# 304 transposes of a decoder layer move from TensorE to VectorE, in squares of 32 by 32

## The chip, the cores and the metric

The kernel runs on one core of a Trainium2 chip. The metric is the device time of one execution in microseconds. In the profile TensorE is PE (its loads of the stationary operand are PEld), VectorE is DVE, ScalarE is ACT, GpSimd is POOL, SyncE is SP.

## What is computed

One decoder layer in float32: 256 tokens, 2048 features, a feed-forward width of 5632, two attentions of 8 heads with 128 features each.

```python
x = x + 0.5 * swiglu(rmsnorm(x, g_ffn1), w_ffn1_gu, w_ffn1_down)
h = rmsnorm(x, g_mix)
qa, ka, va, qb, kb, vb, gate_a, gate_b = split(h @ w_in)
o_a = diff_attention(qa, ka, va)       # attention 1, two softmax maps per head
o_b = moba_attention(qb, kb, vb)       # attention 2; with 256 tokens plain causal attention
merged = sigmoid(gate_a) * (o_a @ p_a) + sigmoid(gate_b) * (o_b @ p_b)
x = x + merged @ w_o
x = x + 0.5 * swiglu(rmsnorm(x, g_ffn2), w_ffn2_gu, w_ffn2_down)
return rmsnorm(x, g_final)
# swiglu(h): gate, up = split(h @ w_gu); (silu(gate) * up) @ w_down
```

## The kernel before

All weights are read once, from DRAM, in pieces `raw` of 512 rows by 512 columns (three buffers). A float32 product is made of three passes of TensorE: a number is split into a high and a low part of 12 bits each, and hi x hi, hi x lo and lo x hi are added up in PSUM. So each piece of weights is split on the chip, two blocks of 128 rows at a time: ACT makes `wh` (line 102), DVE makes `wl` (line 103), each in four buffers. Activations are the stationary operand: 128 features by 128 tokens, split in the same way, and for that they must be transposed, with the features on the partitions.

`products` (line 122) runs one product: for every 128 rows k of the weights and for both token tiles t it issues three matmuls of 512 columns (lines 130 to 132). Its two PSUM tiles `acc` are two of four, so that the next product can run while the last one is read out. For each pair of row blocks PE issues 12 matmuls, ACT one wh, DVE one wl.

What comes out of a product has the tokens on the partitions. To be an operand again it goes through `flipped` (line 172): TensorE transposes four blocks of 128 by 128 into a PSUM tile `tr`, and ACT and DVE split that into the operand. There are three forms. `put` (line 180) writes hi and lo of h (the feed-forward's inner activations, 22 blocks of 512 columns in all) and of mg (the merged attentions, 4 blocks). `put_x` (line 202) does it for x with a gain, 4 blocks for each of three operands. `put_rows` (line 198) writes the queries and keys of an attention (qk, 4 blocks for each), ACT alone. Such a piece of work is for both token tiles, so eight transposes. It isn't done at once: it is put into the queue `work`, and `products` takes one piece out of it after each 512 rows of weights from the second on (line 141). The stages of the attention heads stand in the same queue.

The stages follow each other: the first feed-forward (gate and up of six blocks, a down product over these, five blocks, a down product over those, which also ends each block of x), q, k, v of attention 1, the same of attention 2 with the heads of attention 1 in between, two gates of 2048 columns with the heads of attention 2 in between, then `merged` in 4 blocks (lines 412 to 424: a product with p_a and one with p_b of 8 row blocks each, multiplied by the gates on DVE, line 419, and added, line 423), `w_o` in 4 products (line 425), and the second feed-forward. A block of x is ready when its last product has been added (lines 261 and 428); `after` then queues its transposes.

A scheduler writes each engine's order of instructions before the run, by priorities and by when it expects an instruction to be ready. The splits of weights are given a priority 600 instructions ahead (line 151).

Of the kernel before, what the change touches and what calls it, by code (L numbers as in the profile page):

```python
"""One decoder layer: SwiGLU half-step, differential and MoBA attention in parallel, SwiGLU
half-step, RMSNorm.

Products with weights: a float32 number is the exact sum of two float32r numbers of 12 significant
bits each, so x @ w is hi(x) @ hi(w) + hi(x) @ lo(w) + lo(x) @ hi(w) + lo(x) @ lo(w) with exact
products. The first three are passes of TensorE at its full rate; the last is at most 2**-24 of
each product, under the rounding of a float32 product, as is the error of a product that leaves it
out. Activations are stationary (transposed, 128 tokens by 128), weights stream past them in blocks
of 512 columns, are split on the chip, and each is read from DRAM once.

An RMSNorm's gain is applied as the rows are transposed and its 1/rms to the product, which is
linear in each row.
"""
# [14 lines left out]
ALU = mybir.AluOpType  # L28
# [8 lines left out]
NB = 512  # L37
HEADS = 8
# [8 lines left out]
def layer(ctx: ExitStack, tc: tile.TileContext, x_in, g_ffn1, w_gu1, w_down1, g_mix, w_in, lam_q1,  # L47
# [12 lines left out]
    # the activation functions of the SwiGLU are loaded before anything waits for them  # L60
# [8 lines left out]
    def load_gains(c0, gs):  # L69
        """A column of `gains` for each 128 features of the gains."""  # L70
        n = sum(g.shape[-1] for g in gs) // P
        rows = tp.tile([n, P], F32, name="gain_rows", tag="osq", bufs=1)
        r = 0
        for g in gs:
            m = g.shape[-1] // P
            nc.scalar.dma_start(rows[r:r + m], g[0].rearrange("(k p) -> k p", p=P))
            r += m
        tr = psum.tile([P, n], F32, name="tr_g", tag="tr", bufs=2)
        nc.tensor.transpose(tr, rows, ident[:n, :n])
        return nc.vector.tensor_copy(gains[:, c0:c0 + n], tr).ins  # L80
# [5 lines left out]
    def make_dist():  # L86
        # key position - query position where that is <= 0, a large negative number elsewhere:
        # queries 0..127 with keys 0..127, then queries 128..255 with keys 0..255
        nc.gpsimd.iota(dist[:, :P], pattern=[[1, P]], base=0, channel_multiplier=-1,
                       allow_small_or_imprecise_dtypes=True)  # L90
        nc.gpsimd.iota(dist[:, P:], pattern=[[1, S]], base=-P, channel_multiplier=-1,
                       allow_small_or_imprecise_dtypes=True)
        nc.gpsimd.affine_select(dist[:, :P], dist[:, :P], pattern=[[-1, P]], compare_op=ALU.is_ge, fill=NEG,
                                base=0, channel_multiplier=1)
        nc.gpsimd.affine_select(dist[:, P:], dist[:, P:], pattern=[[-1, S]], compare_op=ALU.is_ge, fill=NEG,
                                base=P, channel_multiplier=1)

# [1 line left out]
    def split(hi, lo, src, scale=None):  # L99
        """src (* scale) as hi + lo, exactly."""  # L100
        if scale is None:
            a = nc.scalar.activation(hi, src, AF.Copy)  # L102
            b = nc.vector.tensor_tensor(lo, src, hi.bitcast(F32), op=ALU.subtract)  # L103
        else:
            a = nc.scalar.activation(hi, src, AF.Copy, scale=scale)  # L105
            b = nc.vector.scalar_tensor_tensor(lo, src, scale, hi.bitcast(F32), op0=ALU.mult, op1=ALU.subtract)
        return a.ins, b.ins

    def after_all(instructions):
        """What follows is issued behind these on their engines."""  # L110
        stack = ExitStack()
        for i in instructions:
            stack.enter_context(tc.issue_after(i))
        return stack
# [7 lines left out]
    def products(lhs, w, starts, nk, before=None, behind=(), apart=0):  # L122
        """For each n0 of starts two PSUM tiles, 128 tokens each: lhs (an operand) @ w[:, n0:n0+512].
        The last `apart` rows of 128 go through TensorE for one token tile, then for the other.
        Other work that waits goes in between, a piece for each 512 rows."""
# [9 lines left out]
        for c in range(0, nk, 4):  # L135
# [6 lines left out]
            for i, (acc, n0) in enumerate(zip(accs, starts)):  # L142
# [5 lines left out]
                for b in range(0, 4, 2):  # L148
                    wh = wp.tile([P, 2, NB], F32R, name="wh", bufs=4)
                    wl = wp.tile([P, 2, NB], F32R, name="wl", bufs=4)  # L150
                    with tc.high_priority(offset=PRIORITY), after_all(begun if c == 0 else ()):
                        pair = split(wh, wl, raw[:, b:b + 2, :])
                    if fill is not None and c == b == i == 0:
                        with after_all(pair):
                            begun.extend(fill())
                    for j in range(2):
                        k = c + b + j
                        last = passes(acc, 0, k, wh[:, j, :], wl[:, j, :])
                        if k < nk - apart:
                            passes(acc, 1, k, wh[:, j, :], wl[:, j, :])  # L160
                        else:
                            later.append((acc, 1, k, wh[:, j, :], wl[:, j, :]))
# [9 lines left out]
    def flipped(src):  # L172
        """[128, up to 4 * 128] in PSUM: each 128 columns of src, transposed."""
# [6 lines left out]
    def put(lhs, k0, srcs):  # L180
        """Columns of the token tiles go transposed, as hi + lo, into an operand."""
        for t, src in enumerate(srcs):
            n = src.shape[-1] // P
            tr = flipped(src).rearrange("p (k q) -> p k q", k=n)
            hi, lo = columns(lhs, k0, n, t)
            split(hi, lo, tr)

    def operand(nk, *tags):
        """Tokens' rows, transposed, in one piece for each tag: (hi, lo), each [128, nk, 256]."""
        return [tuple(keep.tile([P, nk, S], F32R, name=f"{tag}{i}", tag=f"{tag}{i}") for i in "hl") for tag in tags]  # L190

    def columns(lhs, k, n, t):
        """n times 128 columns of a token tile, as hi and lo: [128, n, 128]."""
# [4 lines left out]
    def put_rows(dst, srcs):  # L198
        for t, src in enumerate(srcs):
            nc.scalar.activation(dst[:, :, t * P:(t + 1) * P], flipped(src).rearrange("p (k q) -> p k q", k=4), AF.Copy)  # L200

    def put_x(lhs, n0, g):
        """x[:, n0:n0+512] * gain, transposed."""
# [13 lines left out]
    def inverse_rms(ss):  # L217
        """1 / rms of each row, [128, 1] for each token tile."""
# [14 lines left out]
    def ffn(xT, ss, w_gu, w_down, after, before=None, behind=(), apart=0):  # L233
        rstd = None
        parts = [range(0, 6), range(6, 11)]
        for part, blocks in enumerate(parts):
            hT = operand(24, "big")
            for b in blocks:
# [12 lines left out]
                hs = []  # L251
                for t in range(T):
                    hs.append(tp.tile([P, NB], F32, name="h", tag="h", bufs=2))
                    nc.vector.scalar_tensor_tensor(hs[t], up[t], rstd[t], sg[t], op0=ALU.mult, op1=ALU.mult)
                work.appendleft(partial(put, hT, (b - blocks[0]) * 4, hs))
# [11 lines left out]
    def weights(h, maps, qT, kT):  # L267
        """p: [128, maps, 384], queries 0..127 then 128..255; their sums: [128, 2, maps]."""
# [20 lines left out]
    def flip_weights(a):  # L289
        """[128 keys, 384]: keys 0..127 for all queries, keys 128..255 for queries 128..255."""  # L290
# [4 lines left out]
    def diff_head(h, qT, kT, v, lam, on, oT):  # L295
# [3 lines left out]
        # (p0 - p1 * lam * sum0 / sum1) is the difference of the maps times sum0  # L299
# [46 lines left out]
    def qkv(xT, rstd, n0, dim, tag):  # L346
        """Transposed queries (scaled) and keys [128, head, 256], values [128, token tile, 1024]."""
# [7 lines left out]
        for i, (dst, r) in enumerate(((qT, rq), (kT, rstd))):  # L355
            for b in range(W // NB):
                y = product(xT, w_in[0], n0 + i * W + b * NB, KD)
                hs = []
                for t in range(T):
                    hs.append(tp.tile([P, NB], F32, name="qk", tag="h", bufs=2))  # L360
                    nc.vector.tensor_scalar(hs[t], y[t], r[t], None, op0=ALU.mult)
                work.appendleft(partial(put_rows, dst[:, 4 * b:4 * b + 4], hs))
# [6 lines left out]
    def lam_of():  # L369
# [7 lines left out]
        # -lam  # L377
# [4 lines left out]
    def in_steps(heads):  # L382
        """A stage of each head after the same stage of the head before; a step takes the next stage
        of every head under way."""
# [8 lines left out]
    def mixer(xT, ss, after):  # L393
# [18 lines left out]
        for n0 in range(0, D, NB):  # L412
# [7 lines left out]
            hs = []  # L420
            for t in range(T):
                hs.append(tp.tile([P, NB], F32, name="mg", tag="h", bufs=2))
                nc.vector.tensor_add(hs[t], gates[0][:, t, cols], gates[1][:, t, cols])
            work.appendleft(partial(put, mT, n0 // P, hs))
# [12 lines left out]
    def next_operand(g, nk, *tags):  # L437
        """What the step before fills: the operand, and the sums of squares."""
        lhs, ss = [], square_sums()

        def after(n0):
            if not lhs:
                lhs.extend(operand(nk, *tags))
            sum_squares(ss, n0)
            work.appendleft(partial(put_x, lhs, n0, g))
# [6 lines left out]
    def load_x(k):  # L452
        """Starts the load of 512 columns; the function that puts them into the operand."""
# [69 lines left out]
```

## Time and profile before

| | |
|---|---|
| time, median of 3 runs (lowest to highest) | 2143.42 us (2143.32 to 2143.74) |
| the profiled execution, first to last instruction | 2141.3 us |
| PE, weight loads PEld busy | 2124.6 us, 1760.1 us |
| DVE, ACT busy | 1116.9 us, 981.2 us |
| granted clock of PE, mean | 0.999 of 2.4 GHz |

The numbers come from one profiled execution; the page gives the busy time of each engine and the groups of instructions, and other views of the same trace give them in order of time. A record of PE ends where the last result has left the array, so records of neighbours overlap, and what an instruction costs PE is read from start to start. In a row of a group, the last part is the idle time of the engine just ahead of these instructions and what ended it.

### The profile page before, as it was taken

How to read it: one execution, taken by the hardware profiler on the slowest of the kernel's cores; microseconds unless marked ns; L12 is line 12 of the kernel's file. 1: busy time of each engine (PE TensorE's matmuls, PEld its weight loads, DVE VectorE, ACT ScalarE, POOL GpSimd, SP SyncE). 2: the span in 40 equal slices, each digit the busy share in tenths (PEclk: the TensorE clock that was granted, in tenths of full speed). 3: DMA queues.
4: the chain of work that ended last, by engine and by line, in shares of the span. 5: the costliest groups of instructions: out<-in, count | busy, mean ns of one | idle time of the engine just before them, and what ended most of it. 6: DMA issues, size and time to landing. Idle time of an engine off the chain costs nothing.

```text
span 2141.3 us, 23791 instructions
## 1 busy us (share of the span) xinstructions
PE 2124.6 (99%) x9634; PEld 1760.1 (82%) x9634; DVE 1116.9 (52%) x1238; ACT 981.2 (46%) x1224; POOL 11.7 (1%) x26
## 2 busy tenths in 40 slices
PE   8999999999999999999999999999999999999998
PEld 7888888888888888778888888888888888888886
DVE  5554454454555554665554466555554545445554
ACT  6444433344444444555564544544444433444443
POOL 0000000000000000000000000000000000000000
PEclk9999999999999999999999999999999999999999
DMA  7555555555555555544545555566555555555553
GB/s 259 187 186 195 183 192 197 195 184 191 196 183 191 183 190 178 176 157 158 180 162 189 196 187 187 188 205 196 179 195 190 186 195 196 191 185 195 192 184 136
DMA packets 201792, 401.20 MB, mean 187 GB/s; under 512 B 6945, under 2 KB 6994, under 8 KB 201554
## 3 DMA queue, kind: packets, MB, share of 16 engines
q1 hardware_dynamic: 201584, 399.66, 56.2%
q8 instruction: 75, 1.23, 0.2%
q14 instruction: 35, 0.29, 0.0%
q10 hardware_dynamic: 98, 0.03, 0.0%
HBM read 397.57 MB, written 2.10 MB: 187 GB/s over the span
## 4 chain that ended last, share of the span: by engine, by line
PE 99%; ACT 1%; DMA 0%; DVE 0%; ACTq 0%; issue 0%; SPq 0%; POOLq 0%
PE acc L130 32%; PE acc L132 32%; PE acc L131 32%; PE tr L177 2%; ACT wh L102 0%; DMA raw<-in_w_ffn_gu_dram 0%; PE sc L274 0%; PE o L341 0%; PE sc L272 0%; ACT on L316 0%; ACT oah L105 0%; PE o L342 0%; DVE wl L103 0%; DVE s L277 0%; SPq L456 0%
## 5 line engine op out<-in xcount | busy, mean ns | idle before, releaser
L103 DVE TENSOR_TENSOR wl<-raw,wh 128x1024 fp32r<-128x1024 f32 x752 | 921.3, 1226 | 988.0 <-ACT wh L102 987.6
L102 ACT ACTIVATE wh<-raw 128x1024 fp32r<-128x1024 f32 x752 | 796.7, 1060 | 1070.1 <-PE acc L132 1039.9
L130 PE MATMUL acc<-wh,xTh 128*128 128x512 f32 x1472 | 578.3, 393 | 2.0 <-ACT xTh L105 2.0
L132 PE MATMUL acc<-wh,xTl 128*128 128x512 f32 x1472 | 574.1, 390 | 0.0
L131 PE MATMUL acc<-wl,xTh 128*128 128x512 f32 x1472 | 573.6, 390 | 0.0
L130 PEld LDWEIGHTS acc<-wh,xTh 128*128 128x128 f32 x1472 | 276.9, 188 | 59.4 <-ACT xTh L105 2.4
L132 PEld LDWEIGHTS acc<-wh,xTl 128*128 128x128 f32 x1472 | 276.7, 188 | 58.0
L131 PEld LDWEIGHTS acc<-wl,xTh 128*128 128x128 f32 x1472 | 277.0, 188 | 56.3
L130 PE MATMUL acc<-wh,bigh 128*128 128x512 f32 x704 | 274.5, 390 | 0.0
L132 PE MATMUL acc<-wh,bigl 128*128 128x512 f32 x704 | 274.0, 389 | 0.0
L131 PE MATMUL acc<-wl,bigh 128*128 128x512 f32 x704 | 273.9, 389 | 0.0
L130 PE MATMUL acc<-wh,oah 128*128 128x512 f32 x416 | 163.1, 392 | 0.0
L132 PE MATMUL acc<-wh,oal 128*128 128x512 f32 x416 | 162.0, 390 | 0.0
L131 PE MATMUL acc<-wl,oah 128*128 128x512 f32 x416 | 161.9, 389 | 0.0
L130 PE MATMUL acc<-wh,obh 128*128 128x512 f32 x416 | 161.8, 389 | 0.0
L131 PE MATMUL acc<-wl,obh 128*128 128x512 f32 x416 | 161.8, 389 | 0.0
L132 PE MATMUL acc<-wh,obl 128*128 128x512 f32 x416 | 161.8, 389 | 0.0
L131 PEld LDWEIGHTS acc<-wl,bigh 128*128 128x128 f32 x704 | 132.2, 188 | 27.4
L132 PEld LDWEIGHTS acc<-wh,bigl 128*128 128x128 f32 x704 | 132.1, 188 | 27.4
L130 PEld LDWEIGHTS acc<-wh,bigh 128*128 128x128 f32 x704 | 132.2, 188 | 27.2
L132 PEld LDWEIGHTS acc<-wh,oal 128*128 128x128 f32 x416 | 78.1, 188 | 16.4
L130 PEld LDWEIGHTS acc<-wh,obh 128*128 128x128 f32 x416 | 78.1, 188 | 16.2
(112 smaller groups left out, 927.1 us busy)
## 6 DMA issues: line engine op xcount, KB each, us to landing
raw<-in_w_ffn_gu_dram SPq DMA_DIRECT2D x174, 1024.0 KB, 5.0
raw<-in_w_ffn_down_dram SPq DMA_DIRECT2D x88, 1024.0 KB, 5.0
raw<-in_w_in_dram SPq DMA_DIRECT2D x80, 1024.0 KB, 5.1
raw<-in_w_o_dram SPq DMA_DIRECT2D x16, 1024.0 KB, 5.0
raw<-in_p_a_dram SPq DMA_DIRECT2D x8, 1024.0 KB, 5.1
raw<-in_p_b_dram SPq DMA_DIRECT2D x8, 1024.0 KB, 5.0
x<-in_x_dram SPq DMA_DIRECT2D x8, 256.0 KB, 5.4
raw<-in_w_ffn_gu_dram SPq DMA_DIRECT2D x4, 512.0 KB, 6.1
```

Source lines behind the costliest of these rows:

```text
L102: a = nc.scalar.activation(hi, src, AF.Copy)
L103: b = nc.vector.tensor_tensor(lo, src, hi.bitcast(F32), op=ALU.subtract)
L130: nc.tensor.matmul(acc[t], hi, wh, start=(k == 0), stop=False)
L131: nc.tensor.matmul(acc[t], hi, wl, start=False, stop=False)
L132: return nc.tensor.matmul(acc[t], lo, wh, start=False, stop=(k == nk - 1)).ins
L177: nc.tensor.transpose(tr[:, i * P:(i + 1) * P], src[:, i * P:(i + 1) * P], ident)
```

## The change

`turned` does the transposes of a block of 512 columns on VectorE: 16 instructions, one for each quarter a of the tokens' 128 partitions and each quarter c of the features' 128. Each reads 32 partitions of both token tiles, 256 numbers of each partition, and transposes them in squares of 32 by 32; it writes the 32 partitions of the features. The result `rows` lies in SBUF with its columns in the order a, t, block, token, and the splits read it in an order that puts them right. `turned` is called where the block is made; only the splits wait in `work`. The two token tiles of a block are now one tile `hs` with one buffer, in place of two buffers of one tile each, `rows` has one buffer, and `wl` has three buffers in place of four.

The first operand (the x that is loaded) still goes through `put_x` and TensorE. The queries and keys go through `turned` where nothing waits in `work`, else through `flipped`: at attention 1 the queue is empty, at attention 2 the heads of attention 1 wait in it.

```diff
+Q = 32
...
-                    wl = wp.tile([P, 2, NB], F32R, name="wl", bufs=4)
+                    wl = wp.tile([P, 2, NB], F32R, name="wl", bufs=3)
...
-    def put(lhs, k0, srcs):
-        for t, src in enumerate(srcs):
-            n = src.shape[-1] // P
-            tr = flipped(src).rearrange("p (k q) -> p k q", k=n)
-            hi, lo = columns(lhs, k0, n, t)
-            split(hi, lo, tr)
+    def both_tiles(name):
+        return tp.tile([P, T, NB], F32, name=name, tag="h", bufs=1)
+
+    def turned(both):
+        rows = tp.tile([P, 4, T, 4, Q], F32, name="rows", tag="rows", bufs=1)
+        both = both.rearrange("p t (k c j) -> p c t k j", c=4, j=Q)
+        for a in range(4):
+            for c in range(4):
+                nc.vector.transpose(rows[c * Q:(c + 1) * Q, a], both[a * Q:(a + 1) * Q, c])
+        return rows
+
+    def put(lhs, k0, rows):
+        for t in range(T):
+            hi, lo = (part.rearrange("p k (a i) -> p k a i", i=Q) for part in columns(lhs, k0, 4, t))
+            split(hi, lo, rows[:, :, t].rearrange("p a k i -> p k a i"))
...
+    def put_turned_rows(dst, rows):
+        for t in range(T):
+            nc.scalar.activation(dst[:, :, t * P:(t + 1) * P].rearrange("p k (a i) -> p k a i", i=Q),
+                                 rows[:, :, t].rearrange("p a k i -> p k a i"), AF.Copy)
+
+    def put_turned(lhs, n0, g, rows):
+        for i in range(NB // P):
+            k = n0 // P + i
+            for t in range(T):
+                hi, lo = (part[:, 0].rearrange("p (a i) -> p a i", i=Q) for part in columns(lhs, k, 1, t))
+                split(hi, lo, rows[:, :, t, i], scale=gains[:, g * KD + k:g * KD + k + 1])
...
-                hs = []
-                for t in range(T):
-                    hs.append(tp.tile([P, NB], F32, name="h", tag="h", bufs=2))
-                    nc.vector.scalar_tensor_tensor(hs[t], up[t], rstd[t], sg[t], op0=ALU.mult, op1=ALU.mult)
-                work.appendleft(partial(put, hT, (b - blocks[0]) * 4, hs))
+                hs = both_tiles("h")
+                for t in range(T):
+                    nc.vector.scalar_tensor_tensor(hs[:, t], up[t], rstd[t], sg[t], op0=ALU.mult, op1=ALU.mult)
+                work.appendleft(partial(put, hT, (b - blocks[0]) * 4, turned(hs)))
...
-                work.appendleft(partial(put_rows, dst[:, 4 * b:4 * b + 4], hs))
+                if work:
+                    put_piece = partial(put_rows, dst[:, 4 * b:4 * b + 4], hs)
+                else:
+                    put_piece = partial(put_turned_rows, dst[:, 4 * b:4 * b + 4], turned(hs))
+                work.appendleft(put_piece)
...
-            work.appendleft(partial(put, mT, n0 // P, hs))
+            work.appendleft(partial(put, mT, n0 // P, turned(hs)))
...
+            rows = turned(x[:, :, n0:n0 + NB])
             sum_squares(ss, n0)
-            work.appendleft(partial(put_x, lhs, n0, g))
+            work.appendleft(partial(put_turned, lhs, n0, g, rows))
```

## Rows read from the trace of the kernel before

**Rows 1.** The page: span, busy time of each engine, chain that ended last.

```profile
span 2141.3 us, 23791 instructions
...
PE 2124.6 (99%) x9634; PEld 1760.1 (82%) x9634; DVE 1116.9 (52%) x1238; ACT 981.2 (46%) x1224; POOL 11.7 (1%) x26
...
PE 99%; ACT 1%; DMA 0%; DVE 0%; ACTq 0%; issue 0%; SPq 0%; POOLq 0%
```

**Rows 2.** Groups by line: count | busy us, mean ns | idle before, releaser.

```profile
L103 DVE TENSOR_TENSOR wl<-raw,wh 128x1024 fp32r<-128x1024 f32 x752 | 921.3, 1226 | 988.0 <-ACT wh L102 987.6
L102 ACT ACTIVATE wh<-raw 128x1024 fp32r<-128x1024 f32 x752 | 796.7, 1060 | 1070.1 <-PE acc L132 1039.9 <-issue 18.6 <-ACT sq L215 5.3
```

**Rows 3.** PE in order of time, around eight transposes: start, length, what.

```profile
106.59 0.40 PE L132 MATMUL acc<-wh,xTl 128*128 128x512 f32 x1
106.82 1.04 PE L177 MATMUL tr<-ident,h 128*128 128x128 f32 x8
...
107.93 0.39 PE L131 MATMUL acc<-wl,xTh 128*128 128x512 f32 x1
```

**Rows 4.** Groups by line: PE's transposes that the change touches.

```profile
L177 PE MATMUL tr<-ident,h 128*128 128x128 f32 x176 | 22.8, 272 | 0.0
...
L177 PE MATMUL tr<-ident,x 128*128 128x128 f32 x96 | 13.4, 285 | 0.0
...
L177 PE MATMUL tr<-ident,qk 128*128 128x128 f32 x64 | 8.3, 272 | 0.0
...
L177 PE MATMUL tr<-ident,mg 128*128 128x128 f32 x32 | 4.1, 272 | 0.0
```

**Rows 5.** Groups by line: prices on DVE, and one on ACT.

```profile
L254 DVE SCALAR_TENSOR_TENSOR h<-acc,rstd,sg 128x512 f32<-128x512 f32 x44 | 31.0, 743 | 0.2 <-issue 0.2
...
L103 DVE TENSOR_TENSOR bigl<-tr,bigh 128x512 fp32r<-128x512 f32 x44 | 28.2, 682 | 0.0
...
L106 DVE SCALAR_TENSOR_TENSOR xTl<-tr,gains,xTh 128x128 fp32r<-128x128 f32 x64 | 20.3, 346 | 3.5 <-ACT xTh L105 3.4
...
L416 ACT ACTIVATE gate<-gate 128x512 f32<-128x512 f32 x16 | 10.1, 634 | 0.4
...
L304 DVE SCALAR_TENSOR_TENSOR a<-s,c 128x256 f32<-128x256 f32 x8 | 3.8, 479 | 0.0
...
L103 DVE TENSOR_TENSOR obl<-o,obh 128x256 fp32r<-128x256 f32 x8 | 3.3, 418 | 0.0
...
L335 DVE TENSOR_SCALAR a<-s,inv 128x256 f32<-128x256 f32 x8 | 2.8, 348 | 0.0
```

**Rows 6.** DVE in order of time, an h block.

```profile
99.95 1.23 DVE L103 TENSOR_TENSOR wl<-raw,wh 128x1024 fp32r<-128x1024 f32 x1 [1.50 <-ACT wh L102]
101.09 1.40 DVE L254 SCALAR_TENSOR_TENSOR h<-acc,rstd,sg 128x512 f32<-128x512 f32 x2
102.67 1.23 DVE L103 TENSOR_TENSOR wl<-raw,wh 128x1024 fp32r<-128x1024 f32 x1 [0.18 <-ACT wh L102]
```

**Rows 7.** DVE in order of time, end of an mg block.

```profile
1267.04 1.28 DVE L419 TENSOR_TENSOR gate<-acc,gate 128x512 f32<-128x512 f32 x2
1268.23 0.68 DVE L423 TENSOR_TENSOR mg<-gate,gate 128x512 f32<-128x512 f32 x1
1268.83 1.22 DVE L103 TENSOR_TENSOR wl<-raw,wh 128x1024 fp32r<-128x1024 f32 x1
1269.97 0.69 DVE L423 TENSOR_TENSOR mg<-gate,gate 128x512 f32<-128x512 f32 x1
```

**Rows 8.** All engines in order of time, one weight pair in w_o.

```profile
1327.36 1.06 ACT L102 ACTIVATE wh<-raw 128x1024 fp32r<-128x1024 f32 x1 [1.66 <-PE acc L132]
...
1328.45 1.23 DVE L103 TENSOR_TENSOR wl<-raw,wh 128x1024 fp32r<-128x1024 f32 x1 [1.50 <-ACT wh L102]
```

**Rows 9.** Stretches of mg, w_o: length, busy (x instructions), PEclk, DMA share.

```profile
1240.00:1320.00 80.00, 80.00 (x371) 66.56 (x370) 51.35 (x57) 33.75 (x37) 0.00 (x0) 1.00 0.55 188
1320.00:1410.00 90.00, 90.00 (x415) 74.85 (x414) 51.74 (x70) 45.68 (x73) 1.08 (x2) 1.00 0.59 198
```

More of the change, by code (lines that the diff above doesn't have):

```diff
@@ L196, in columns, with put_rows @@
         return [part[:, k:k + n, t * P:(t + 1) * P] for part in lhs[i]]
-    def put_rows(dst, srcs):
-        for t, src in enumerate(srcs):
-            nc.scalar.activation(dst[:, :, t * P:(t + 1) * P], flipped(src).rearrange("p (k q) -> p k q", k=4), AF.Copy)
+    def put_rows(dst, both):
+        for t in range(T):
+            nc.scalar.activation(dst[:, :, t * P:(t + 1) * P],
+                                 flipped(both[:, t]).rearrange("p (k q) -> p k q", k=4), AF.Copy)
+    def put_turned_rows(dst, rows):
[8 more added lines that the diff above has]
+                split(hi, lo, rows[:, :, t, i], scale=gains[:, g * KD + k:g * KD + k + 1])
     def put_x(lhs, n0, g):
@@ L357, in qkv @@
                 y = product(xT, w_in[0], n0 + i * W + b * NB, KD)
-                hs = []
+                hs = both_tiles("qk")
                 for t in range(T):
-                    hs.append(tp.tile([P, NB], F32, name="qk", tag="h", bufs=2))
-                    nc.vector.tensor_scalar(hs[t], y[t], r[t], None, op0=ALU.mult)
-                work.appendleft(partial(put_rows, dst[:, 4 * b:4 * b + 4], hs))
+                    nc.vector.tensor_scalar(hs[:, t], y[t], r[t], None, op0=ALU.mult)
+                if work:
[3 more added lines that the diff above has]
+                work.appendleft(put_piece)
         for b in range(W // NB):
@@ L419, in mixer @@
                     nc.vector.tensor_mul(g[:, t, cols], y[t], g[:, t, cols])
-            hs = []
+            hs = both_tiles("mg")
             for t in range(T):
-                hs.append(tp.tile([P, NB], F32, name="mg", tag="h", bufs=2))
-                nc.vector.tensor_add(hs[t], gates[0][:, t, cols], gates[1][:, t, cols])
-            work.appendleft(partial(put, mT, n0 // P, hs))
+                nc.vector.tensor_add(hs[:, t], gates[0][:, t, cols], gates[1][:, t, cols])
+            work.appendleft(partial(put, mT, n0 // P, turned(hs)))
         for n0 in range(0, D, NB):
```

## The prediction

> **What bounds the kernel now.** I read the first line of the page first: PE is busy 99% of the span, DVE about half, ACT less than half, and the chain of work that ended last is PE for 99% of it [rows 1]. A busy PE need not be a bound, so the next view is who waits for whom in the groups by line: ACT's split of the weights (wh) sat idle 1070 us and nearly all of that ended when PE finished a matmul, and DVE's split (wl) sat idle 988 us waiting for ACT's wh [rows 2]. So both producers stand ahead of PE, held back by their buffers. Time that leaves PE's stream is gained, as long as nobody else becomes late.
>
> The beat of the kernel is one pair of 128 weight rows: wl starts every 2.72 us (99.95 to 102.67, [rows 6]) and PE spends 12 matmuls on it (2 rows, 2 token tiles, 3 passes), so a matmul costs 2.72 / 12 = 0.227 us of PE's stream, although its record says 0.39.
>
> **What is removed.** The trap is the record's duration here too. A transpose is recorded with 272 ns [rows 4], and 304 of those would be 83 us. But they overlap. In PE's timeline, the last matmul before a group of eight starts at 106.59 and the second one behind it at 107.93 [rows 3]: 1.34 us, of which two matmuls are 2 x 0.227 = 0.45. Eight transposes, with the slow first matmul behind them, cost 0.885 us of the stream. The change removes all of h (176), all of mg (32), half of qk (32 of 64; attention 2's calls find work waiting and stay on PE), and of x the two later operands (64 of 96) [rows 4]: 304, or 38 groups of eight. **38 x 0.885 = 33.6 us**. It is the largest gain that this edit can bring. The 2.1 us between the span (2141.3) and the median (2143.4) I leave as they are.
>
> **What is added on DVE.** Each of the 38 groups becomes 16 transposes on VectorE (4 quarters of the tokens by 4 of the features), each on 32 partitions and 256 elements of each (2 token tiles, 4 blocks, 32 columns): 608 instructions. None is in the trace, so their price is bounded by rows. From below: the cheapest row with 256 elements, the scaled copy, 348 ns, less the overlap of neighbours (two h instructions of 743 ns take 1.40 together [rows 5, 6], so 0.09 can be hidden): 0.26. From above: the row with twice the elements, 682 ns, which is a transpose that needs two steps per element. The rows nearest in size at one element a step are 418 and 479 ns [rows 5]. I take 0.45, between these two, and take no overlap off, since no row shows neighbours on different partitions. A group is 16 x 0.45 = 7.2 us, all 608 are 274 us, and DVE would go from 1117 to about 1390 us, 65%.
>
> The Trainium skill speaks against the change at this point ("VectorE: DVE Perf Modes", section "Two Vector instructions with no wait between them"): a Vector instruction whose input or output starts in another quadrant of 32 partitions than the one before starts only when all earlier ones have finished. Neighbours here do change quadrant. By that rule the 0.09 is not to be had and 0.45 stands; without it, 0.36. No run so far shows it; which one holds decides between my forecast and the first rival. The same page ("The three transpose paths") has 311 ns for 128 columns of 16-bit data; an estimate from it with 128 more elements at 0.96 GHz is 311 + 133 = 444 ns.
>
> Other parts with one answer: the splits now read SBUF and not PSUM. On ACT that is 634 ns (gate, from SBUF) for the 512 elements; on DVE 682 from either memory [rows 5, 7]. ACT is idle more than half the time and hides it. PSUM tiles and waits of the transposes go; nobody waits for them. No DMA is added and no queue is passed.
>
> **Where DVE's work meets PE.** In a beat of 2.72 us DVE has 2.72 - 1.23 = 1.49 us free. The order on DVE puts a wl in wherever it is due: one stands between the two mg additions [rows 7]. So transposes should fill the gaps, about three in each, and a group is spread over five beats. A wl can be late by how much? Today ACT starts a wh when PE releases the oldest of four [rows 8], 1.09 and 1.23 us later wl is ready, and PE wants it three beats and a matmul after the release: 8.39 - 2.32 = 6.1 us to spare. **wl has three buffers instead of four** after the change: DVE starts when PE leaves the third last, and 2 x 2.72 + 0.23 - 1.23 = 4.4 us are left. With gaps filled one instruction at a time that covers any delay (0.45 us at most), so this edit costs nothing. If the cover is gone it is rival 3.
>
> Most groups (22 of h) have two products of 16 rows, 43 us, for 7.2: hidden. But four stages are dense. I count DVE per block against PE's time.
> - *mg, 4 blocks of 8 beats, 21.8 us.* Eight wl 9.84, four products with the gates 2.72, two additions 1.36, transposes 7.2, two lo parts 1.36: 22.5. Now 51.35 of 80 us [rows 9] are busy; after it DVE is over-full by 0.7 a block, 2.8 us in all. PE feels it because the evictions of `acc` (four PSUM tiles, so two products) are queued behind the transposes on DVE.
> - *mg to w_o.* The last block is first used at row 12 of the next product, six beats or 16.3 us after the block's last matmul. In that time DVE has six wl 7.4, two products with the gate 1.36, two additions 1.36, transposes 7.2, ACT's hi 0.63, a lo 0.68: 18.6, so 2.3 us late.
> - *w_o, 4 products of 8 beats.* 9.84 + two additions 1.36 + 7.2 + eight lo 2.8 (0.35 each [rows 5]) = 21.2 of 21.8: just fits. At its end the last x block is needed at row 12 of the first gate product: 7.4 + 1.36 + 7.2 + about 0.4 + 0.35 = 16.7 against 16.3; 0.4 us, with one transpose in the way about 1.
> - *First feed-forward's end to the mixer.* The down products have 10 beats, 27.2 us, for 12.3 + 1.36 + 7.2 + 2.8 = 23.7: fits. The same joint at the end: about 1.
> - *qk of attention 1.* 9.84 + 1.48 + 7.2 = 18.5 of 21.8: fits, and its reader comes later.
>
> Stalls: 2.8 + 2.3 + 1 + 1 = **7 us**. Forecast: 2143.4 - 33.6 + 7 = **2117 us**.
>
> **Rivals.**
> 1. *DVE hides everything.* With 0.36 a group is 1.44 us shorter: mg has 21.1 of 21.8, and the joint to w_o is 0.9 late, the others on time. About 1.5 us of stalls: **2111**. For it: every neighbouring pair on DVE in the trace overlaps [rows 6]. Against: they all start on the same partition.
> 2. *DVE becomes the bound in the dense stages.* At 0.68 a group takes 10.9 us, 3.7 more. mg: 26.2 of 21.8, 4 x 4.4 = 17.6; its joint 6.0; w_o 24.9, 4 x 3.1 = 12.4; two joints 4.1 each; down products 0.2 x 4; qk 0.4 x 4. Sum 46.6: **2156**, slower. Between 7 us at 0.45 and 46.6 at 0.68 the stalls eat the 33.6 us at about **0.60 us a transpose**: from there it decides. For it: a transpose of 4-byte numbers is in no row. Against: every DVE row with 128x1024 and 128x512 goes at one element a step (1226 and 682, 1.06 ns an element).
> 3. *The sixteen transposes stand in a lump on DVE.* Then 7.2 us lie between two wl, the gap has 1.49 and the buffers 4.4: 1.3 us late, and 2.7 with the two h in front; for 38 groups 49 to 103 us: **2159 to 2213**, slower. Against: [rows 7].
> 4. *The transposes were not in PE's way,* and the time stays at **2143**, because a wl or a DMA would have been late. Against: DMA engines are busy 0.55 to 0.59 in the densest stages [rows 9], and PE waits for neither.
>
> **How the numbers follow.** Chances: forecast 0.62 (0.40 to 0.52 us a transpose, 2112 to 2127), rival 1 0.18, rival 2 0.10, rival 3 0.05, rival 4 0.05. The range goes from rival 1 with 2 us for what was rounded, 2109, up to a price just short of the turning point, 2137; what lies above is rivals 2 to 4, at most 0.2. A measurement of this kernel can tell 0.2% (4.3 us) from no change: faster than 2139 takes the forecast, rival 1 and a part of rival 2 under 0.60 (0.02): 0.82. Within 0.2%: rival 4: 0.05. Slower: rivals 2 and 3: 0.13.
>
> **What would show it.** PE: 128 transposes left, no h and no mg among them; two matmuls next to a former group 0.227 apart. DVE: 608 new instructions at 0.45, busy near 1390. PE idle before passes with wl: none beside the h blocks (rival 3 if there is), and before mT's third block and the first xT or oa/ob operand some 1 to 3 us each; PE idle at the start of a p_a or w_o product, with the eviction as the cause, of some 3 us in all. If the transposes come at 0.36, stalls nearly vanish; at 0.6 and more the stages from mg to w_o take as long as DVE needs. The forecast is wrong if wl's are late outside the dense stages, or if the order on DVE holds something back that I took as filled in.

## The result, and the profile after

The changed kernel takes **2110.95 us** (median of 4 runs, 2110.02 to 2111.54) against 2143.58 us before: a ratio of 0.9847, with a 95% interval of 0.9833 to 0.9861, 32.6 us less. The forecast was 2117 us, 26 us less, with a range of 2109 to 2137.

The page of the changed kernel, answering to [rows 1]: span, busy time, and the chain that ended last.

```profile
span 2109.7 us, 24363 instructions
...
PE 2091.8 (99%) x9330; PEld 1729.4 (82%) x9330; DVE 1380.0 (65%) x1846; ACT 983.5 (47%) x1224; POOL 13.6 (1%) x26
...
PE 98%; ACT 1%; DVE 0%; DMA 0%; issue 0%; ACTq 0%; SPq 0%; POOLq 0%; POOL 0%; DVEq 0%
```

PE has 304 matmuls fewer (9634 to 9330), and the profiled execution is 31.6 us shorter (2141.3 to 2109.7); DVE has 608 instructions more and 263 us more to do. PE is busy 99% as before.

Groups by line and shape of the changed kernel, answering to [rows 2, 4, 5]; the columns are count | busy us, mean ns of one | idle before, releaser.

```profile
L104 DVE TENSOR_TENSOR wl<-raw,wh 128x1024 fp32r<-128x1024 f32 x752 | 918.1, 1224 | 619.7 <-PE acc L132 558.2 <-issue 39.8 <-ACT wh L103 10.8
...
L193 DVE STREAM_TRANSPOSE rows<-h 32x256 f32<-32x256 f32 x352 | 153.5, 436 | 6.4
...
L193 DVE STREAM_TRANSPOSE rows<-x 32x256 f32<-32x256 f32 x128 | 55.8, 436 | 2.3
...
L193 DVE STREAM_TRANSPOSE rows<-qk 32x256 f32<-32x256 f32 x64 | 27.9, 436 | 1.1
L193 DVE STREAM_TRANSPOSE rows<-mg 32x256 f32<-32x256 f32 x64 | 27.9, 436 | 1.0
...
L178 PE MATMUL tr<-ident,x 128*128 128x128 f32 x32 | 5.1, 311 | 0.0
...
L178 PE MATMUL tr<-ident,qk 128*128 128x128 f32 x32 | 4.1, 272 | 0.0
```

352 + 128 + 64 + 64 are the 608 transposes, 436 ns each. Of PE's transposes of x and qk, 32 each are left; h and mg are gone. DVE's wl now waits mostly for PE, no longer for ACT: a wl buffer has become what it stands behind.

Who waited for whom on PE, in the changed kernel (us in total, times, longest):

```profile
PE acc L131 <- ACT xTh L106: 2.2, 1, 2.2
PE tr L178 <- ACT on L343: 1.5, 5, 0.3
PE tr L178 <- DVE a L331: 0.4, 1, 0.4
PE acc L133 <- DVE xTl L104: 0.2, 1, 0.2
```

The first two lines were there before, with 2.0 and 1.5 us: the start, and the heads of attention 1. The third, also beside the heads, is the same 0.4 us in the first run below, which has no transposes on DVE. Only the last line can come from them: 0.2 us, where the forecast had 7 us of stalls. This is the question of the experiments: why does PE feel nothing of 608 instructions that the count in the prediction saw over-fill two stages?

### The profile page after: what moved, and what is told of

It is laid out like the page before. It is cut to its first block, busy times and chain, and to the rows that moved or that the text cites. A ratio compares the mean times of both kernels' runs of the same rounds, so it can differ in the third digit from the quotient of the medians.

```text
span 2109.7 us, 24363 instructions
## 1 busy us (share of the span) xinstructions
PE 2091.8 (99%) x9330; PEld 1729.4 (82%) x9330; DVE 1380.0 (65%) x1846; ACT 983.5 (47%) x1224; POOL 13.6 (1%) x26
## 4 chain that ended last, share of the span: by engine, by line
PE 98%; ACT 1%; DVE 0%; DMA 0%; issue 0%; ACTq 0%; SPq 0%; POOLq 0%; POOL 0%; DVEq 0%
PE acc L131 32%; PE acc L133 32%; PE acc L132 32%; PE tr L178 1%; ACT wh L103 0%; DMA raw<-in_w_ffn_gu_dram 0%; PE sc L301 0%; PE o L368 0%; DVE wl L104 0%; PE sc L299 0%; ACT on L343 0%; ACT oah L106 0%; PE o L369 0%; ACT sq L243 0%; DVE rows L193 0%
## 5 line engine op out<-in xcount | busy, mean ns | idle before, releaser
L193 DVE STREAM_TRANSPOSE rows<-h 32x256 f32<-32x256 f32 x352 | 153.5, 436 | 6.4
L133 PEld LDWEIGHTS acc<-wh,obl 128*128 128x128 f32 x416 | 78.1, 188 | 16.2
```

Source lines behind the costliest of these rows:

```text
L133: return nc.tensor.matmul(acc[t], lo, wh, start=False, stop=(k == nk - 1)).ins
L193: nc.vector.transpose(rows[c * Q:(c + 1) * Q, a], both[a * Q:(a + 1) * Q, c])
```

## Experiments

**What the transposes cost, all together.** The 608 transposes are left out; `turned` hands on the block untransposed, only read in another order:

```diff
-        rows = tp.tile([P, 4, T, 4, Q], F32, name="rows", tag="rows", bufs=1)
-        both = both.rearrange("p t (k c j) -> p c t k j", c=4, j=Q)
-        for a in range(4):
-            for c in range(4):
-                nc.vector.transpose(rows[c * Q:(c + 1) * Q, a], both[a * Q:(a + 1) * Q, c])
-        return rows
+        return both.rearrange("p t (k a i) -> p a t k i", a=4, i=Q)
```

> The changed kernel without its 608 transposes on VectorE: the splits read the tiles untransposed, so what is computed with is wrong; all else is as in the changed kernel. Theory A (the transposes are hidden: each takes 0.45 us of VectorE, and what they delay is covered by the lead of wl): the time falls by the 0.5 us that PE lost at mT, to about 2110 us (2109 to 2111). Theory B (the sum of the prediction, 7 us of stalls by the transposes): 2104 us.

Measured: 2110.22 us (2109.38 to 2111.09), 0.5 to 0.7 us under the changed kernel (which took 2110.71 in a second measurement), as theory A has it. That is less than executions of one kernel differ by, so the traces have to tell where it lies. From the first matmul of a stage to the first of the next, both kernels take the same to 0.02 us in all stages but two: w_o, 87.57 us with the transposes and 87.04 without, and the first gate and up products, where the number of slow matmuls at the start differs (13 and 6, see the end). So 263 us of work on DVE cost the kernel 0.5 us.

**Is it the lead of wl that hides them?** One number is changed, in the changed kernel (three buffers) and in the kernel before (four):

```diff
-                    wl = wp.tile([P, 2, NB], F32R, name="wl", bufs=3)
+                    wl = wp.tile([P, 2, NB], F32R, name="wl", bufs=2)
```

> The changed kernel with two wl buffers in place of three. Theory A: wl runs late behind every group of transposes, by some 2.2 us of a lead of 4.4 us in the trace; two buffers leave a lead of 2.72 + 0.23 - 1.23 = 1.7 us, so each of the 38 groups comes 0.5 us short: up to 20 us, 2125 to 2131 us, less if the scheduler orders it anew. Rival A2 (VectorE has room and the lead isn't needed): 2111 us.

> The kernel before with two wl buffers in place of four, as the control. The longest work that stands on VectorE between two wl of the dense blocks is 1.4 us, in a gap of 1.49 us, so a lead of 1.7 us is enough except beside the attention heads: theory A 2143 to 2148 us. If two buffers cost as much here as in the changed kernel, the transposes are not what needs the lead.

Measured: the changed kernel rises to 2139.33 us (2138.65 to 2140.22), 28.4 us more and above the 2125 to 2131 us expected; the kernel before to 2144.48, 0.8 us more, a ratio of 1.0004 (0.9994 to 1.0014). So the transposes are what needs the lead, as theory A has it, but each of the 38 groups costs 0.75 us and not 0.5. The waits for wl of PE's weight loads, and PE around one group in order of time, with two buffers:

```profile
PEld acc L132 <- DVE wl L104: 38.3, 86, 0.7
```

```profile
112.26 0.39 PE L131 MATMUL acc<-wh,xTh 128*128 128x512 f32 x1
112.72 0.50 PE L132 MATMUL acc<-wl,xTh 128*128 128x512 f32 x1
113.06 0.40 PE L133 MATMUL acc<-wh,xTl 128*128 128x512 f32 x1
...
115.38 0.39 PE L131 MATMUL acc<-wh,xTh 128*128 128x512 f32 x1
115.80 0.50 PE L132 MATMUL acc<-wl,xTh 128*128 128x512 f32 x1
```

There are 86 waits, against one of 0.4 us in the changed kernel; how much of these 38.3 us PE loses shows in its starts alone. Around this group two matmuls with wl start 0.2 us late (0.46 and 0.42 behind their neighbours in place of 0.23), and the one behind each is 0.1 late once more: some 0.6 of the 0.75 us. Without the third buffer 28.4 of the 32.6 us would be lost.

**What if a transpose cost more?** Five of sixteen are done twice:

```diff
-                nc.vector.transpose(rows[c * Q:(c + 1) * Q, a], both[a * Q:(a + 1) * Q, c])
+                for _ in range(2 if a == c or (a, c) == (0, 1) else 1):
+                    nc.vector.transpose(rows[c * Q:(c + 1) * Q, a], both[a * Q:(a + 1) * Q, c])
```

> The changed kernel with 5 of each 16 transposes done twice: a group takes 9.45 us of VectorE, as if a transpose took 0.59 us. Theory A, from what VectorE does in the changed kernel (21.5 us of 21.76 in an mg block, 20.0 in a w_o product): mg is 2 us over in each of 4 blocks, w_o 0.45 in each of 4 products, the three joints 1 to 2 us each: 2123 us (2118 to 2130). Theory B (the sum of the prediction, interpolated at 0.59): 31 us of stalls, 2141 us. Rival A2 (room left): 2111 us.

Measured: 2132.55 us (2132.35 to 2132.94), between the two theories and above the range of theory A. Compared with the changed kernel, the stages are longer by 2.0 us (q, k, v of attention 1), 3.1 us (mg), 11.1 us (w_o) and 5.0 us (second feed-forward's first products); a joint counts to the stage behind it. They were to be 1 to 2, 8, 3 to 4, and 1 to 2 us. PE's waits, and three stretches (length, busy time and instructions of PE, PEld, DVE, ACT, POOL, granted clock, DMA share, GB/s) at the beginning of w_o:

```profile
PE acc L131 <- ACT xTh L103: 5.7, 1, 5.7
...
PE acc L131 <- ACT obh L106: 3.0, 1, 3.0
...
PE acc L132 <- DVE wl L104: 1.9, 5, 0.5
```

```profile
1316.20:1322.20 6.00, 0.35 (x2) 0.00 (x0) 5.75 (x11) 0.67 (x2) 0.00 (x0) 0.92 0.44 148
1322.20:1328.00 5.80, 5.79 (x14) 4.59 (x15) 1.75 (x3) 1.43 (x2) 0.00 (x0) 0.50 0.40 154
1328.00:1334.00 6.00, 6.00 (x28) 4.93 (x27) 4.49 (x5) 3.46 (x5) 0.00 (x0) 1.00 0.49 169
```

At the joint from mg to w_o PE waits 5.7 us for one operand. By the sums, this is where most of what DVE is over in four blocks of mg falls due: 8 us were expected in mg, and 3.1 came there. And then PE's clock is granted at 0.50, half of 2.4 GHz, until about 1328: the next matmuls start 0.43 us apart and not 0.23, some 3 us more. The wait of 3.0 us at the joint behind w_o is followed by slow matmuls too. Such a wait on PE is dearer than its length. The run also shows that the kernel was near an edge: 2.25 us more in each group cost 21.6 us, while the first 7.2 us in each group had cost 0.5 us in the whole kernel.

**Does a change of partitions keep neighbours apart?** Each transpose is cut in two, so that each second one stays on the same 32 partitions:

```diff
-                nc.vector.transpose(rows[c * Q:(c + 1) * Q, a], both[a * Q:(a + 1) * Q, c])
+                for t in range(T):
+                    nc.vector.transpose(rows[c * Q:(c + 1) * Q, a, t], both[a * Q:(a + 1) * Q, c, t])
```

> The changed kernel with each transpose cut in two, one for each token tile: 32 of 128 elements in a group, and each second one reads and writes the same 32 partitions as the one before it. Theory H (a change of partitions keeps a transpose from starting before the one ahead has ended): starts alternate, about 0.32 us where the partitions change behind it and 0.22 us (0.303 less the 0.09 that neighbours overlap) where they do not; a group takes 8.6 us in place of 7.2. Rival H2 (a transpose never overlaps its neighbour): 0.32 us throughout, 10.1 us a group. Time: 1.4 us more in each group, 0.6 of what the kernel with 21 transposes adds, so 2115 to 2126 us; with H2 2130 us and more.

Measured: 2117.46 us (2117.32 to 2117.95). DVE in order of time, in an h block:

```profile
104.90 1.23 DVE L104 TENSOR_TENSOR wl<-raw,wh 128x1024 fp32r<-128x1024 f32 x1
106.16 2.02 DVE L194 STREAM_TRANSPOSE rows<-h 32x128 f32<-32x128 f32 x8
108.21 1.23 DVE L104 TENSOR_TENSOR wl<-raw,wh 128x1024 fp32r<-128x1024 f32 x1
```

Eight take 2.02 us, one in 0.255 on average. One by one, the starts alternate: 0.236 us from the first of a pair to the second, which is on the same partitions and starts 66 ns before the first has ended; 0.274 us to the next pair, which starts 14 ns after the end. Theory H, with a smaller step than expected (0.22 and 0.32). In the changed kernel all 456 neighbouring pairs are of the second kind and start 0.450 us apart, 436 + 14 ns. The rule of the Trainium skill ("VectorE: DVE Perf Modes", section "Two Vector instructions with no wait between them") held for these pairs. The time fits too: a group takes 16 x 0.51 = 8.2 us, and at the joint from mg to w_o PE waits again, now 3.5 us:

```profile
1315.28 0.77 PE L131 MATMUL acc<-wh,xTh 128*128 128x512 f32 x1 [3.48 <-ACT xTh L103]
```

**The dense stages undone.** The 12 groups of mg and x go back to TensorE (`put_flipped` splits from `flipped(both[:, t])`):

```diff
-            work.appendleft(partial(put, mT, n0 // P, turned(hs)))
+            work.appendleft(partial(put_flipped, mT, n0 // P, hs))
...
-            rows = turned(x[:, :, n0:n0 + NB])
...
-            work.appendleft(partial(put_turned, lhs, n0, g, rows))
+            work.appendleft(partial(put_x, lhs, n0, g))
```

> The changed kernel with the 12 groups of mg and x back on TensorE; h and the queries and keys of attention 1 stay on VectorE. Theory A (a group of eight costs TensorE 0.885 us and these 12 cost it 0.5 us as transposes on VectorE): 2111 + 10.6 - 0.5 = 2121 us. Theory B (7 us of stalls come from these groups): 2111 + 10.6 - 7 = 2114.6 us.

Measured: 2121.1 us (2120.82 to 2121.24). Theory A to 0.1 us, and theory B, the prediction's count, is 6.5 us off. It also confirms the price of eight transposes on PE by itself: (2121.1 - 2110.95 + 0.5) / 12 = 0.888 us.

**More of the same.** The last TensorE transposes of queries and keys go to VectorE, then three of the four blocks of the first x too:

```diff
-                if work:
-                    put_piece = partial(put_rows, dst[:, 4 * b:4 * b + 4], hs)
-                else:
-                    put_piece = partial(put_turned_rows, dst[:, 4 * b:4 * b + 4], turned(hs))
+                put_piece = partial(put_turned_rows, dst[:, 4 * b:4 * b + 4], turned(hs))
...
-                done = put_x(first, n0, 0)
+                done = put_x(first, n0, 0) if k == 0 else put_turned(first, n0, 0, turned(x[:, :, n0:n0 + NB]))
```

> The changed kernel with the queries and keys of attention 2 on VectorE too: 4 groups more leave TensorE, 4 x 0.885 = 3.5 us. Theory A (VectorE is busy 99.6 of 157 us there, 28.8 more fit): 2107.5 us (2107 to 2109). Rival C (the heads of attention 1 run there, each step waits for VectorE, and a group of 7.2 us delays them until TensorE waits): 2111 us or more.

> As the run with both queries and keys, and three of the four blocks of the first x on VectorE too (the very first block stays on TensorE): another 3 x 0.885 = 2.7 us. Theory A: 2105 us (2104 to 2107). Rival C2 (in the first 40 us x is still arriving and VectorE makes wl for two products, so its operand comes late): 2108 us or more.

Measured: 2121.35 us (2120.24 to 2121.89), 10.4 us more where 3.5 less was expected, and 2138.97 us (2137.24 to 2140.43), another 17.6 us more. That is the side of rivals C and C2, and far beyond the 2111 and 2108 us that they began at. PE's waits in the stage of the heads with both queries and keys on VectorE, and the stretch behind one of them (columns as above):

```profile
PE tr L178 <- ACT on L343: 8.1, 5, 2.6
PE tr L178 <- DVE on L351: 1.9, 1, 1.9
```

```profile
914.00:919.00 5.00, 5.00 (x15) 3.94 (x14) 3.37 (x12) 2.36 (x9) 0.69 (x1) 0.50 0.24 93
```

In the changed kernel PE waits 1.9 us in this stage; here 10.3 us, four of the waits near 2 us or above, and three are followed by matmuls at half the clock. On DVE the 16 transposes of a block stand ahead of the heads' next steps, with only wl between them. With the first x too, PE waits four times for it, where the changed kernel has one wait of 2.2 us:

```profile
PE acc L131 <- ACT xTh L106: 14.4, 4, 4.5
```

Two ways to let the heads go first were tried:

```diff
+                if work:
+                    with tc.high_priority(offset=-150):
+                        rows = turned(hs)
```

> The queries and keys of attention 2 on VectorE as in the run with both, but their 64 transposes with a priority 150 instructions lower, so that the heads' steps go first on VectorE. If the loss of that run came from the heads waiting behind the transposes (theory C), most of it is gone: 2108 to 2114 us, at best 3.5 us under the changed kernel. If VectorE has no room there at all (rival D), as before, 2121 us.

```diff
+                if work:
+                    work.insert(2, lambda to=to, hs=hs: put_turned_rows(to, turned(hs)))
```

> The same, with the priority as it was, but the 16 transposes of a block are queued as a piece of work behind two steps of the heads, at the last 512 rows of the next product, and not at once. Theory C: the two steps ahead are no longer held up, 2108 to 2116 us. Rival D: 2121 us.

and the changed kernel beside them, unaltered:

> The changed kernel itself, on the chip of the next two runs: 2111 us (2110 to 2111.6).

Measured: 2121.82 us (2120.97 to 2122.58) and 2121.62 us (2121.02 to 2121.74), and 2110.71 us (2110.47 to 2111.21) for the changed kernel. Neither gives anything back. But the lower priority is no test of the order: in the trace of that run every engine has the same instructions in the same order as with both queries and keys on VectorE. The later place in the queue does change the order, DVE's transposes then stand between the heads' steps, one to five at a time. PE's waits in the stage are 10.8 us in all, and most of them are for another step of the heads:

```profile
PE tr L178 <- DVE a L331: 9.0, 4, 5.0
```

So theory C is neither confirmed nor refuted. Which step of the heads' chain (DVE, ACT and PE take turns in it) sets the time, and if another order could save it, stays open. Of the versions that leave nothing out, none is faster than the changed kernel.

## Why the prediction was right, and where its sum was not

The mechanism was right: what leaves PE's stream is gained, and DVE takes it over in its gaps. The number was right with some luck: 2111 us lies below the 2112 to 2127 us that the forecast kept for itself, and inside the range because the range began at rival 1.

*The gain on PE* was right: 38 x 0.885 = 33.6 us. Of it 32.6 came through; 0.5 us is the wait before w_o, and the rest is no more than the start of an execution varies by. Reading the starts and not the records (272 ns each, 83 us) decided this.

*The price of a transpose* was right: 0.45 us predicted, 0.436 recorded and 0.450 from start to start; DVE busy 1380 us where 1390 was forecast. Rival 1 gave 2111 us, the measured time, but for a reason that is wrong: it had 0.36 us by overlap, and there is none between transposes.

*The step that failed is the count of the dense stages*: 7 us of stalls, measured 0.5. It set every other DVE instruction at its recorded duration. DVE in order of time in the changed kernel, one mg block from additions to additions:

```profile
1252.57 1.28 DVE L452 TENSOR_TENSOR mg<-gate,gate 128x512 f32<-128x512 f32 x2
1253.77 1.22 DVE L104 TENSOR_TENSOR wl<-raw,wh 128x1024 fp32r<-128x1024 f32 x1
1254.91 1.77 DVE L193 STREAM_TRANSPOSE rows<-mg 32x256 f32<-32x256 f32 x4
1256.71 1.23 DVE L104 TENSOR_TENSOR wl<-raw,wh 128x1024 fp32r<-128x1024 f32 x1
1257.97 2.23 DVE L193 STREAM_TRANSPOSE rows<-mg 32x256 f32<-32x256 f32 x5
1260.23 1.23 DVE L104 TENSOR_TENSOR wl<-raw,wh 128x1024 fp32r<-128x1024 f32 x1
1261.49 1.79 DVE L193 STREAM_TRANSPOSE rows<-mg 32x256 f32<-32x256 f32 x4
1263.30 1.23 DVE L104 TENSOR_TENSOR wl<-raw,wh 128x1024 fp32r<-128x1024 f32 x1
1264.56 1.34 DVE L193 STREAM_TRANSPOSE rows<-mg 32x256 f32<-32x256 f32 x3
1265.94 0.69 DVE L449 TENSOR_TENSOR gate<-acc,gate 128x512 f32<-128x512 f32 x1
1266.54 1.22 DVE L104 TENSOR_TENSOR wl<-raw,wh 128x1024 fp32r<-128x1024 f32 x1
1267.68 1.29 DVE L104 TENSOR_TENSOR xTl<-rows,xTh 128x512 fp32r<-128x512 f32 x2
1268.88 0.68 DVE L449 TENSOR_TENSOR gate<-acc,gate 128x512 f32<-128x512 f32 x1
1269.48 2.35 DVE L104 TENSOR_TENSOR wl<-raw,wh 128x1024 fp32r<-128x1024 f32 x2
1271.99 0.69 DVE L449 TENSOR_TENSOR gate<-acc,gate 128x512 f32<-128x512 f32 x1 [0.16 <-PE acc L133]
1272.60 1.22 DVE L104 TENSOR_TENSOR wl<-raw,wh 128x1024 fp32r<-128x1024 f32 x1
1273.73 0.68 DVE L449 TENSOR_TENSOR gate<-acc,gate 128x512 f32<-128x512 f32 x1
1274.33 1.28 DVE L452 TENSOR_TENSOR mg<-gate,gate 128x512 f32<-128x512 f32 x2
```

The block takes 1274.33 - 1252.57 = 21.76 us, PE's eight beats, with 0.16 us idle. From start to start:

| | prediction, us | measured, us |
|---|---|---|
| eight wl | 9.84 | 9.54 |
| four products with the gates | 2.72 | 2.41 |
| two additions | 1.36 | 1.20 |
| two lo | 1.36 | 1.20 |
| sixteen transposes | 7.2 | 7.25 |
| sum | 22.5 | 21.60 |

The prediction knew the overlap of 0.09 us (from two h instructions) and refused it to the transposes, rightly, but did not grant it to the sixteen others. Thirteen of them have it; the three wl that take 1.26 us stand ahead of a transpose that starts on other partitions. That is 0.9 us a block, and the stage fits with 0.16 us to spare: 0 in place of 2.8 us.

*The joint from mg to w_o*, forecast 2.3 us late. PE in order of time in the changed kernel:

```profile
1310.55 0.39 PE L131 MATMUL acc<-wh,xTh 128*128 128x512 f32 x1
1310.78 0.39 PE L132 MATMUL acc<-wl,xTh 128*128 128x512 f32 x1
1311.34 0.50 PE L133 MATMUL acc<-wh,xTl 128*128 128x512 f32 x1 [0.17 <-DVE xTl L104]
```

0.33 us late, at the third pass. From the first product with the gate (1293.75) to the end of the first lo (1311.28) DVE takes 17.5 us and not 18.6, again by overlap. It starts 0.45 us before the stage begins (1294.2), since the first token tile's sum is done three matmuls ahead of the second's. And lo is wanted only by the third pass, two matmuls or 0.45 us after hi. 18.6 - 1.1 - 0.45 - 0.45 is 16.6 against 16.3. The two other joints, forecast at 1 us each, show no wait: their stages take 130.56 and 261.12 us with the transposes and without.

*The three buffers of wl* cost nothing, as forecast, but not because a gap is filled one instruction at a time. DVE in order of time, an h block of the changed kernel, answering to [rows 6]:

```profile
104.89 1.23 DVE L104 TENSOR_TENSOR wl<-raw,wh 128x1024 fp32r<-128x1024 f32 x1
106.15 2.23 DVE L193 STREAM_TRANSPOSE rows<-h 32x256 f32<-32x256 f32 x5
108.41 1.22 DVE L104 TENSOR_TENSOR wl<-raw,wh 128x1024 fp32r<-128x1024 f32 x1
```

Five transposes stand between two wl, 2.25 us in a gap of 1.49, so each wl comes 3.5 us after the last and not 2.72. At the end of a group it is 2.2 us late: of 4.4 us to spare (the count was right) 2.2 are left, at worst 1.6. The lump of rival 3 was there in part, and the buffers paid for it; with two buffers it costs 28 us.

*The turning point* was set too low: at 0.59 us a transpose the prediction's sum gives 2141 us, and the run with 21 of them, which takes as much of DVE, 2132.5 us.

## What to carry to other kernels

An engine that is busy 99% gives back what is taken from it, start to start, if the engine that takes the work over has gaps and its consumer has a lead to lend: count the lead in buffers, and see how much of it is left after the change, since it ends suddenly. When stages are nearly full, add up instructions from start to start, with the overlap that neighbours on the same partitions have and those on different ones have not. The last stretch of moving work is the risky one: the next four groups, each the same 0.885 us on PE, were to save 3.5 us and lost 10.4.

## What was not expected of the hardware

After a wait PE can come back at half the clock: matmuls 0.43 us apart at a granted clock of 0.50 followed the waits of 5.66 us (21 transposes) and 3.48 us (halves), and in the heads of attention 1, with queries and keys on VectorE, those of 2.62, 2.63 and 1.85 us; they did not follow one of 2.24 us there, nor the 0.33 us of the changed kernel. The length of the wait alone does not decide it: in the run with the lower priority, with the same order of instructions, a wait of 2.25 us at the same place was followed by seven such matmuls. What does decide these runs don't tell. At the start, PE's first matmuls are 0.43 us apart in every run, but how many of them varies without a change in what is run: 13 and 11 in two executions of the changed kernel, 7 in the kernel before, 5 to 13 in the others. At 0.2 us each this moves the time by up to 1.6 us, more than the transposes cost.
